# Gathering the next expert's tokens one weight pair earlier and transposing them one pair later

## The chip, the cores and the metric

The kernel runs on one core of a Trainium2 chip. The metric is the device time of one execution in microseconds. The engines are TensorE (PE, with its weight loads as PEld), VectorE (DVE), ScalarE (ACT), GpSimd (POOL) and SyncE (SP), which issues most of the transfers.

## What is computed

One layer of a backbone over 2048 latent tokens and 256 context tokens of width 1024: a mixing sub-layer (a gated convolution beside a bidirectional mLSTM) and then a mixture of 16 experts in which every expert chooses its own 256 tokens. Only the second part matters here; the whole is in float32.

```python
def one_set(hs):                       # hs: (2048, 1024)
    aff = jax.nn.softmax(jnp.einsum('nd,de->en', hs, w_router).astype(jnp.float32), axis=0)
    g, idx = lax.top_k(aff, cap)       # cap = 256 tokens per expert
    xe = hs[idx]
    a = jnp.einsum('ecd,edf->ecf', xe, w_gate)
    u = jnp.einsum('ecd,edf->ecf', xe, w_up)
    ye = jnp.einsum('ecf,efd->ecd', jax.nn.silu(a) * u, w_down) * g[..., None].astype(hs.dtype)
    return jax.ops.segment_sum(ye.reshape(-1, hs.shape[-1]), idx.reshape(-1), num_segments=n)
```

The sum over experts is gated, added to the stream, and a final RMSNorm follows.

## The kernel before

The first stage ends with the normalised tokens and their router weights in a table in memory, XN (2048 rows of 1040 numbers), the stream in ACC, and two small tables, AH and RB, from which the list of an expert's 256 tokens can be made. That takes until about 1160 us. Then the loop over the 16 experts runs, `for e in range(NE)`, with an inner loop over six pairs of 128-wide slices of the expert's hidden width (1408 = 11 slices; the last pair has one).

In each pair, gate and up weights are loaded by SP (load_w, L85), split into a high part on ACT (L92) and a rest on VectorE (L96) and multiplied with the expert's transposed tokens, xh and xl, by 96 matmuls of 256 columns (L1148 to L1150, into psx). The down weights are loaded and split likewise (L1045, L1051, L1053). The 24 down matmuls (L1086 to L1088, into ac) run one pair behind: those of pair 0 are traced in iteration pr = 1, and those of the last pair in pr = 0 of the next expert, followed by finish(), which scales the rows and adds them to ACC by two indirect transfers on POOL's queue (L1110).

While expert e is computed, xprep(e + 1) prepares the next one:

- the one-hot tile oh from ix and AH on VectorE (L1006), 16 index products on TensorE into pi (L1009), a copy to ic (L1011) and the integer indices idx (L1014);
- two indirect gathers from XN into the two tiles gx, 128 rows each, on POOL's queue (L1017);
- the router weights gg from the gathered rows on VectorE (L1021);
- four groups of four transposes on TensorE into ptx (L1032), each group read by ACT (xh, L1035) and VectorE (xf, L1037; xl, L1038), two times in turn.

The PSUM pool ptr has one buffer, which pi and the four groups ptx share. The tile oh has one buffer as well, and the squares eq of early() and finish() use it too (tag "oh"). early(t) normalises rows of ACC that no later expert touches; it runs in the last two experts from pr = 1 on, two row tiles in each pair of expert 14.

The order on each engine isn't written by hand. A planner lays out the instructions by their simulated readiness, and among those that are ready the one traced first goes first; the engines then keep to that order. So the trace place of a call is its priority. All of xprep(e + 1) is called at the end of pr = 2, behind the down matmuls of pair 1:

```python
                if pr == 2 and e + 1 < NE:
                    nxt = xprep(e + 1)
```

Of the kernel before, what the change touches and what calls it, by code (L numbers as in the profile page):

```python
# [25 lines left out]
NE = 16  # L26
# [12 lines left out]
def kernel(ctx, tc, x, c, cx, c_ctx, w_mod, b_mod, g_norm1, g_norm2, w_in, w_out, conv_w, conv_b,  # L39
# [43 lines left out]
    def load_w(src, rows, cols):  # L83
        raw = wrawp.tile([P, rows, cols], F32, name="wraw", tag="wraw")
        nc.sync.dma_start(raw, src)  # L85
        return raw

    def split_w(raw, rows, cols, after=None, after_lo=None):
        hi = whip.tile([P, rows, cols], F32R, name="whi", tag="whi")
        if after is not None:  # L90
            S.activation(hi[:, 0, 0:1], after, AF.Copy)
        S.activation(hi, raw, AF.Copy)  # L92
        lo = whip.tile([P, rows, cols], F32R, name="wlo", tag="wlo")
        if after_lo is not None:
            V.tensor_copy(lo[:, 0, 0:1], after_lo)
        V.tensor_sub(lo, raw, hi.bitcast(F32))  # L96
        return hi, lo
# [150 lines left out]
    for q in range(4):  # L248
        pmf = psm.tile([P, 512], F32, name="pm", tag="sm")
        pm = pmf[:, 0:8].rearrange("p (r i s) -> p r i s", r=2, i=2)  # L250
        for r in range(2):
            pr = pmm.tile([P, 512], F32, name="pr", tag="mm")
# [743 lines left out]
    with tc.tile_pool(name="xw", bufs=2, reuse_waits="tile") as xraw, tc.tile_pool(name="xh", bufs=2, reuse_waits="tile") as xhi, \  # L996
# [2 lines left out]
            tc.tile_pool(name="extr", bufs=1, space=PSUM, reuse_waits="tile") as ptr, \  # L999
            tc.tile_pool(name="exac", bufs=4, space=PSUM, reuse_waits="tile") as pac:  # L1000

        def xprep(e):
            oh = wk.tile([P, P, 16], BF16, name="oh", bufs=1)
            if e == 1:
                V.tensor_copy(oh[:, 0, 0:1], xp[1].bitcast(F32)[:, KD - 1, 0:1])
            V.tensor_tensor(oh, ix, AH[:, e].unsqueeze(1).to_broadcast([P, P, 16]), op=ALU.is_equal)  # L1006
            pi = ptr.tile([P, 512], F32, name="pi", tag="tr")
            for j in range(16):
                T.matmul(pi[:, 0:4], oh[:, :, j], RB[:, e, j], start=j == 0, stop=j == 15)  # L1009
            ic = wk.tile([P, 4], F32, name="ic", bufs=1)  # L1010
            V.tensor_copy(ic, pi[:, 0:4])  # L1011
            idx = wk.tile([P, 2], I32, name="idx", bufs=3)
            icv = ic.rearrange("p (h f) -> p f h", f=2)
            V.scalar_tensor_tensor(idx[:, ::-1], icv[:, 0], float(P), icv[:, 1], op0=ALU.mult, op1=ALU.add)  # L1014
            gxs = [wk.tile([P, XW], F32, name="gx", bufs=2) for _ in range(2)]
            for hf_ in range(2):
                G.indirect_dma_start(out=gxs[hf_], out_offset=None, in_=XN,  # L1017
                                     in_offset=bass.IndirectOffsetOnAxis(ap=idx[:, hf_:hf_ + 1], axis=0))
            gg = wk.tile([P, 2], F32, name="gg", bufs=2)
            for hf_ in range(2):  # L1020
                V.tensor_copy(gg[:, hf_:hf_ + 1], gxs[hf_][:, D + e:D + e + 1])  # L1021
            xh = wk.tile([P, KD, 2 * P], F32R, name="xh", bufs=2)
            xl = wk.tile([P, KD, 2 * P], F32R, name="xl", bufs=2)
            for k2 in range(KD // 2):
                if e == 0:
                    pt = pac.tile([P, 512], F32, name="ac", tag="ac").rearrange("p (i t) -> p i t", i=2)
                else:
                    pt = ptr.tile([P, 2, 2 * P], F32, name="ptx", tag="tr")
                for i in range(2):
                    for hf_ in range(2):  # L1030
                        k = k2 * 2 + i
                        T.transpose(pt[:, i, hf_ * P:(hf_ + 1) * P], gxs[hf_][:, k * P:(k + 1) * P], ident)  # L1032
                for i in range(2):
                    k = k2 * 2 + i
                    S.activation(xh[:, k], pt[:, i], AF.Identity, scale=A2[:, k:k + 1], bias=B2[:, k:k + 1])  # L1035
                    xf = wk.tile([P, 2 * P], F32, name="xf", bufs=2)
                    V.tensor_scalar(xf, pt[:, i], A2[:, k:k + 1], B2[:, k:k + 1], op0=ALU.mult, op1=ALU.add)  # L1037
                    V.tensor_sub(xl[:, k], xf, xh.bitcast(F32)[:, k])  # L1038
            return xh, xl, gg, idx

        def wsplit_d(src, rows, gate=None, after=None, col=None):
            raw = xraw.tile([P, rows, D], F32, name="draw", tag="draw")
            if gate is not None:
                V.tensor_copy(raw[:, 0, 0:1], gate)
            nc.sync.dma_start(raw, src)  # L1045
            if col is not None:
                G.tensor_mul(raw, raw, col.unsqueeze(1).to_broadcast([P, rows, D]))
            hi = xhi.tile([P, rows, D], F32R, name="dhi", tag="dhi")
            if after is not None:
                S.activation(hi[:, 0, 0:1], after, AF.Copy)  # L1050
            S.activation(hi, raw, AF.Copy)  # L1051
            lo = xhi.tile([P, rows, D], F32R, name="dlo", tag="dlo")
            V.tensor_sub(lo, raw, hi.bitcast(F32))  # L1053
            return hi, lo
# [61 lines left out]
                V.tensor_scalar(ar, ar, fr, None, op0=ALU.mult)  # L1116
                G.indirect_dma_start(out=out, out_offset=rows(e, hf_), in_=ar, in_offset=None)

        xp = xprep(0)
        pend = []  # L1120
        for e in range(NE):
            xh, xl, gg, idx = xp
            accs = None
            nxt = None
            for pr in range(npair):
                n = 2 if pr < npair - 1 else NFT - 2 * (npair - 1)
                f0 = pr * 2
                ws = []
                for src in (w_gate_e, w_up_e):
                    raw = load_w(src[0, e][:, f0 * P:(f0 + n) * P].rearrange("(k p) n -> p k n", p=P), KD, n * P)  # L1130
                    if e == 0 and pr == 0:
                        ws.append(split_w(raw, KD, n * P, thr[:, 0:1], idx[:, 0:1]))
                    elif e == 0 and pr == 1 and not ws:
                        ws.append(split_w(raw, KD, n * P, xl.bitcast(F32)[:, 5, 0:1]))
                    else:
                        ws.append(split_w(raw, KD, n * P))
                dw = wsplit_d(w_down_e[0, e][f0 * P:(f0 + n) * P, :].rearrange("(i p) n -> p i n", p=P), n,
                              gg[:, 0:1] if e == 0 and pr < 2 else None,
                              xl.bitcast(F32)[:, KD - 1, 0:1] if e == 0 and pr < 2 else None,
                              ml5b if e == NE - 1 else None)  # L1140
                hts = []
                for i in range(n):
                    ps = pmm.tile([P, 2, 2 * P], F32, name="psx", tag="mm")
                    for m_ in range(2):
                        hi, lo = ws[m_]
                        for k in range(KD):
                            wh = hi[:, k, i * P:(i + 1) * P]
                            T.matmul(ps[:, m_], wh, xh[:, k], start=k == 0, stop=False)  # L1148
                            T.matmul(ps[:, m_], wh, xl[:, k], start=False, stop=False)  # L1149
                            T.matmul(ps[:, m_], lo[:, k, i * P:(i + 1) * P], xh[:, k], start=False, stop=k == KD - 1)  # L1150
                    sgt = wk.tile([P, 2 * P], F32, name="sgt", bufs=2)
                    S.activation(sgt, ps[:, 0], AF.Silu)  # L1152
                    V.tensor_tensor(sgt, ps[:, 1], sgt, op=ALU.mult)  # L1153
                    hh = wk.tile([P, 2 * P], F32R, name="hh", bufs=4)
                    S.activation(hh, sgt, AF.Copy)  # L1155
                    hl = wk.tile([P, 2 * P], F32R, name="hl", bufs=4)
                    V.tensor_sub(hl, sgt, hh.bitcast(F32))  # L1157
                    hts.append((hh, hl))
                last = pr == npair - 1
                if pend and not (e == NE - 1 and last):  # L1160
                    pe, pxp, paccs, ppr, plast = pend.pop()
                    if paccs is None:
                        paccs = [pac.tile([P, 512], F32, name="ac", tag="ac") for _ in range(4)]
                    down(paccs, ppr)
                    if plast:
                        finish(pe, pxp, paccs)
                    else:
                        accs = paccs
                pend.append((e, xp, accs, ([f0 + i for i in range(n)], hts, dw), last))
                if e >= NE - 2 and pr:  # L1170
                    cuts = ((0, 2, 4, 6, 8, 10), (10, 12, 14, 16, 16, 16))[e - NE + 2]
                    for t in range(cuts[pr - 1], cuts[pr]):
                        early(t)
                if pr == 2 and e + 1 < NE:
                    nxt = xprep(e + 1)
            if nxt is not None:
                xp = nxt
        accs = pend[0][2]
# [51 lines left out]
```

## Time and profile before

| | |
|---|---|
| time before, median of 3 runs | 2762.28 us (2760.39 to 2766.7) |
| span of the profiled execution | 2763.4 us |
| TensorE busy | 2641.4 us (96%) |
| VectorE busy | 1605.3 us (58%) |
| ScalarE busy | 1149.4 us (42%) |
| GpSimd busy | 333.2 us (12%) |
| mean granted TensorE clock | 0.983 |

The time of the profiled execution is given by its span; it lies between the fastest and the slowest run shown. Busy times are of one execution. A matmul's listed duration is longer than its share of TensorE's time, since matmuls overlap: what one costs is read from the starts of the ones that follow. A wait is written behind a row as the idle time of its engine and what ended it.

### The profile page before, as it was taken

The numbers are of one execution on the slowest core, as the hardware profiler recorded it, in microseconds if no ns is written. First come the engines' busy times: TensorE is split into PE (matmuls) and PEld (weight loads), VectorE is DVE, ScalarE is ACT, GpSimd is POOL, SyncE is SP. The second block draws the span as 40 slices with busy tenths as digits, with TensorE's granted clock in tenths as the row PEclk, the third lists the DMA queues.
The fourth block names the chain that finished last, engine by engine and source line by source line (L and its number), as shares of the span: only waits on it lengthen the run. The fifth ranks groups of instructions, "written<-read, shape, count | busy, mean of one in ns | idle before, by whom it ended". The sixth has DMA issues, their size and how long they took to land. (4 is left out here: it accounts for less than half of the span.)

```text
span 2763.4 us, 42877 instructions
## 1 busy us (share of the span) xinstructions
PE 2641.4 (96%) x17550; PEld 2378.9 (86%) x17550; DVE 1605.3 (58%) x2603; ACT 1149.4 (42%) x1682; POOL 333.2 (12%) x351
## 2 busy tenths in 40 slices
PE   8999999999999999299999999999999999999987
PEld 5988888888878888299899999999999999999887
DVE  5356454544575665665556555655665565565684
ACT  3243323423434434254444444444444444444443
POOL 1010000000111111300010001001000100100253
PEclk9999999999999999699999999999999999999999
DMA  8444645535565654167567666756756665665965
GB/s 265 134 154 145 188 140 175 183 107 178 201 209 185 200 178 149 61 218 225 176 191 221 194 196 202 219 190 191 221 184 197 207 208 193 198 214 178 304 229 185
DMA packets 382533, 524.57 MB, mean 190 GB/s; under 512 B 15072, under 2 KB 322736, under 8 KB 380288
## 3 DMA queue, kind: packets, MB, share of 16 engines
q1 hardware_dynamic: 327968, 437.96, 48.8%
q10 hardware_dynamic: 43792, 46.55, 5.0%
q0 software_dynamic: 10576, 37.32, 4.9%
q8 instruction: 137, 2.24, 0.3%
q14 instruction: 60, 0.49, 0.1%
HBM read 449.05 MB, written 72.61 MB: 189 GB/s over the span
## 5 line engine op out<-in xcount | busy, mean ns | idle before, releaser
L1148 PE MATMUL psx<-xh,whi 128*128 128x256 f32 x2816 | 793.6, 282 | 0.0
L1150 PE MATMUL psx<-xh,wlo 128*128 128x256 f32 x2816 | 789.4, 280 | 1.3 <-DVE wlo L96 1.3
L1149 PE MATMUL psx<-xl,whi 128*128 128x256 f32 x2816 | 787.8, 280 | 2.1 <-DVE xl L1038 2.1
L96 DVE TENSOR_TENSOR wlo<-wraw,whi 128x2048 fp32r<-128x2048 f32 x248 | 542.1, 2187 | 343.9 <-ACT whi L92 343.7
L92 ACT ACTIVATE whi<-wraw 128x2048 fp32r<-128x2048 f32 x248 | 447.2, 1804 | 394.4 <-PE psx L1149 135.8
L1148 PEld LDWEIGHTS psx<-xh,whi 128*128 128x128 f32 x2816 | 532.1, 189 | 3.2
L1149 PEld LDWEIGHTS psx<-xl,whi 128*128 128x128 f32 x2816 | 530.1, 188 | 5.5 <-DVE xl L1038 2.3
L1150 PEld LDWEIGHTS psx<-xh,wlo 128*128 128x128 f32 x2816 | 530.9, 189 | 2.0 <-DVE wlo L96 1.9
L1088 PE MATMUL ac<-dhi,hl 128*128 128x512 f32 x704 | 278.0, 397 | 4.3 <-DVE hl L1157 4.3
L1086 PE MATMUL ac<-dhi,hh 128*128 128x512 f32 x704 | 278.3, 395 | 0.0
L1087 PE MATMUL ac<-dlo,hh 128*128 128x512 f32 x704 | 278.0, 395 | 0.0
L1053 DVE TENSOR_TENSOR dlo<-draw,dhi 128x2048 fp32r<-128x2048 f32 x96 | 202.7, 2112 | 126.3 <-ACT dhi L1051 126.3
L417 PE MATMUL ps<-hlo,whi 128*128 128x512 f32 (+1 forms) x672 | 259.4, 387 | 0.0
L418 PE MATMUL ps<-hhi,wlo 128*128 128x512 f32 (+1 forms) x672 | 258.9, 386 | 0.0
L416 PE MATMUL ps<-hhi,whi 128*128 128x512 f32 (+1 forms) x672 | 258.4, 387 | 0.0
L1051 ACT ACTIVATE dhi<-draw 128x2048 fp32r<-128x2048 f32 x96 | 170.1, 1773 | 84.0 <-PE ac L1088 84.0
L1110 POOL DMA_INDIRECT ACC<-yv,idx x28 | 82.2, 2937 | 938.9 <-DVE yv L1105 825.8
L1155 ACT ACTIVATE hh<-sgt 128x256 fp32r<-128x256 f32 x176 | 73.1, 417 | 268.3 <-DVE sgt L1153 268.3
L1088 PEld LDWEIGHTS ac<-dhi,hl 128*128 128x128 f32 x704 | 132.2, 188 | 36.8 <-DVE hl L1157 4.5
L1152 ACT ACTIVATE sgt<-psx 128x256 f32<-128x256 f32 x176 | 65.7, 374 | 222.9 <-PE psx L1150 222.9
L1087 PEld LDWEIGHTS ac<-dlo,hh 128*128 128x128 f32 x704 | 132.3, 188 | 28.2
L1086 PEld LDWEIGHTS ac<-dhi,hh 128*128 128x128 f32 x704 | 132.3, 188 | 28.1
(405 smaller groups left out, 3981.7 us busy)
## 6 DMA issues: line engine op xcount, KB each, us to landing
wraw<-in_w_gate_e_dram SPq DMA_DIRECT2D x80, 1024.0 KB, 5.9
wraw<-in_w_up_e_dram SPq DMA_DIRECT2D x80, 1024.0 KB, 5.5
draw<-in_w_down_e_dram SPq DMA_DIRECT2D x80, 1024.0 KB, 5.1
wraw<-in_w_in_dram SPq DMA_DIRECT2D x56, 1024.0 KB, 5.4
pk<-PK SPq DMA_DIRECT2D x16, 1284.0 KB, 7.6
xt<-in_x_dram SPq DMA_DIRECT2D x32, 512.0 KB, 5.3
wraw<-in_w_mod_dram SPq DMA_DIRECT2D x16, 1024.0 KB, 6.9
wm<-in_w_mod_dram SPq DMA_DIRECT2D x8, 1024.0 KB, 12.0
```

The source lines that it names most:

```text
L92: S.activation(hi, raw, AF.Copy)
L96: V.tensor_sub(lo, raw, hi.bitcast(F32))
L416: T.matmul(ps[:, :ntok], wh, his[k], start=k == 0, stop=False)
L417: T.matmul(ps[:, :ntok], wh, los[k], start=False, stop=False)
L418: T.matmul(ps[:, :ntok], lo[:, k, i * P:(i + 1) * P], his[k], start=False, stop=k == KD - 1)
L1053: V.tensor_sub(lo, raw, hi.bitcast(F32))
L1086: T.matmul(ac, hhs, dh[:, i, sl], start=f == 0, stop=False)
L1087: T.matmul(ac, hhs, dl[:, i, sl], start=False, stop=False)
L1088: T.matmul(ac, hls, dh[:, i, sl], start=False, stop=f == NFT - 1)
L1148: T.matmul(ps[:, m_], wh, xh[:, k], start=k == 0, stop=False)
L1149: T.matmul(ps[:, m_], wh, xl[:, k], start=False, stop=False)
L1150: T.matmul(ps[:, m_], lo[:, k, i * P:(i + 1) * P], xh[:, k], start=False, stop=k == KD - 1)
```

## The change

The function xprep is cut in two. xgather(e) holds the one-hot tile, the index products, the indices, the two gathers and the allocation of gg; xprep(e, gth) holds the gg copies, the transposes and their evictions. In the loop xgather(e + 1) is called at the end of pr = 1 and xprep(e + 1, gth) at the end of pr = 3, in place of both at the end of pr = 2. Expert 0 is prepared ahead of the loop by the two calls in a row.

```diff
-        def xprep(e):
+        def xgather(e):
             oh = wk.tile([P, P, 16], BF16, name="oh", bufs=1)
...
             gg = wk.tile([P, 2], F32, name="gg", bufs=2)
+            return gxs, gg, idx
+
+        def xprep(e, gth):
+            gxs, gg, idx = gth
             for hf_ in range(2):
                 V.tensor_copy(gg[:, hf_:hf_ + 1], gxs[hf_][:, D + e:D + e + 1])
...
-        xp = xprep(0)
+        xp = xprep(0, xgather(0))
...
-                if pr == 2 and e + 1 < NE:
-                    nxt = xprep(e + 1)
+                if pr == 1 and e + 1 < NE:
+                    gth = xgather(e + 1)
+                if pr == 3 and e + 1 < NE:
+                    nxt = xprep(e + 1, gth)
```

## Rows read from the trace of the kernel before

**Rows 1.** The page's busy line: engine, busy us, share, instructions.
```profile
PE 2641.4 (96%) x17550; PEld 2378.9 (86%) x17550; DVE 1605.3 (58%) x2603; ACT 1149.4 (42%) x1682; POOL 333.2 (12%) x351
```

**Rows 2.** Waits from 1190 us on: engine, line, releaser: us, times, longest.
```profile
PE ptx L1032 <- DMA gx<-XN,idx: 19.1, 13, 2.8
PE pi L1009 <- DVE oh L1006: 5.0, 1, 5.0
PE psx L1149 <- DVE xl L1038: 2.1, 1, 2.1
PE ptx L1032 <- DVE xf L1037: 1.1, 1, 1.1
...
ACT xh L1035 <- DVE xf L1037: 74.1, 52, 3.1
```

**Rows 3.** TensorE in order of time, one expert: start, us, line, operation, [idle before].
```profile
1709.76 1.15 PE L1009 MATMUL pi<-Cb,oh 128*128 128x4 bf16 x16
...
1719.48 0.30 PE L1032 MATMUL ptx<-ident,gx 128*128 128x128 f32 x1 [1.03 <-DMA gx<-XN,idx]
...
1723.84 0.40 PE L1086 MATMUL ac<-dhi,hh 128*128 128x512 f32 x1
...
1729.44 0.28 PE L1148 MATMUL psx<-xh,whi 128*128 128x256 f32 x1
...
1747.12 0.60 PE L1032 MATMUL ptx<-ident,gx 128*128 128x128 f32 x4
...
1758.59 0.28 PE L1148 MATMUL psx<-xh,whi 128*128 128x256 f32 x1
```

**Rows 4.** Windows: us, busy PE PEld DVE ACT POOL, PEclk, DMA, GB/s.
```profile
1661.84:1673.14 11.30, 11.30 (x97) 11.30 (x96) 3.97 (x5) 4.63 (x4) 0.00 (x0) 1.00 0.65 214
...
2489.00:2504.00 15.00, 13.07 (x98) 12.89 (x97) 5.71 (x8) 4.20 (x7) 3.95 (x2) 0.89 0.33 117
...
2597.00:2607.00 10.00, 10.00 (x70) 10.00 (x71) 5.26 (x8) 3.57 (x5) 3.04 (x5) 0.66 0.83 289
```

**Rows 5.** POOL in order of time: the second scatter and the first gather.
```profile
1687.42 2.78 POOL L1110 DMA_INDIRECT ACC<-yv,idx  x1 [7.78 <-DMA ACC<-yv,idx]
1713.11 2.30 POOL L1017 DMA_INDIRECT gx<-XN,idx  x1 [22.90 <-issue]
```

**Rows 6.** TensorE, ACT and VectorE in order of time, iteration 14.
```profile
2569.94 0.28 PE L1148 MATMUL psx<-xh,whi 128*128 128x256 f32 x1
...
2575.38 1.06 ACT L1062 ACTIVATE eq<-ea 128x1024 bf16<-128x1024 f32 x1 [8.72 <-DMA ea<-ACC]
...
2577.73 0.19 ACT L1062 ACTIVATION_READ_ACCUMULATOR eq<-ea 128x1 f32 x1
...
2578.70 0.42 DVE L1157 TENSOR_TENSOR hl<-sgt,hh 128x256 fp32r<-128x256 f32 x1
...
2595.67 1.22 DVE L1006 TENSOR_TENSOR oh<-ix,UA 128x2048 bf16<-128x2048 bf16 x1
```

**Rows 7.** ACT and VectorE in order of time: reading the last two groups.
```profile
1741.86 0.55 DVE L1037 TENSOR_SCALAR xf<-ptx,A,B 128x256 f32<-128x256 f32 x1 [0.17 <-ACT xh L1035]
...
1750.12 0.56 ACT L1035 ACTIVATE xh<-ptx,B,A 128x256 fp32r<-128x256 f32 x1 [1.30 <-DVE xf L1037]
...
1751.30 0.43 DVE L1038 TENSOR_TENSOR xl<-xf,xh 128x256 fp32r<-128x256 f32 x1
```

**Rows 8.** TensorE in order of time, expert 0: first and last group.
```profile
1225.76 0.60 PE L1032 MATMUL ptx<-ident,gx 128*128 128x128 f32 x4
...
1252.23 0.60 PE L1032 MATMUL ptx<-ident,gx 128*128 128x128 f32 x4
```

**Rows 9.** TensorE in order of time, expert 14: first and last group.
```profile
2613.00 0.27 PE L1032 MATMUL ptx<-ident,gx 128*128 128x128 f32 x1
...
2644.91 0.60 PE L1032 MATMUL ptx<-ident,gx 128*128 128x128 f32 x4
```

**Rows 10.** VectorE in order of time: a weight split late in expert 14.
```profile
2642.47 6.26 DVE L96 TENSOR_TENSOR wlo<-wraw,whi 128x2048 fp32r<-128x2048 f32 x1
```

## The prediction

> **What bounds the kernel now.** I read the page's busy line first, then the waits of TensorE, then the order of time on TensorE inside one expert. The busy line [rows 1] shows TensorE at work for 2641.4 of 2763.4 us and no other engine above 58%, so the kernel gains only what TensorE loses by waiting, about 122 us in all. The waits from 1190 us on, where the expert loop lies [rows 2], tell which part of that this change can touch: 13 waits of the transposes L1032 for the gathered rows (DMA into gx), 19.1 us together, and one wait of the index product L1009 for the one-hot tile oh, 5.0 us. The wait for xl (2.1 us) and that for xf (1.1 us) belong to the same preparation and show what it costs when it comes too late.
>
> The order of time in the expert that prepares from 1709.76 us on [rows 3] shows where the wait comes from. The 16 index products stand right after the down matmuls traced in the third pair; 96 gate and up matmuls of the fourth pair follow, but 63 of them in, at 1719.48, TensorE stands for 1.03 us because the first row tile hasn't landed. The planner had expected it sooner: the gather is issued at 1713.11 [rows 5] and the wait ends at 1719.48, 6.4 us later, while the 63 matmuls fill 7.4 us from the index products' end on. The down matmuls of the fourth pair end at 1729.44, the four groups of transposes reach until 1747.12, and the next expert begins at 1758.59.
>
> **The change part by part.** Nothing is computed more or less: per expert the same 16 index products, two copies to ic and idx, two gathers, two gg copies, 16 transposes, 8 ACT and 16 VectorE evictions. Only the trace place moves, and the place gives the priority by which the planner orders each engine. I take both moves to show in the engines' orders, since the index products stand right behind the down matmuls after which they are traced [rows 3].
>
> *The gather, one pair earlier.* A pair takes 96 matmuls, 11.30 us [rows 4], and 24 down matmuls, 1729.44 - 1723.84 = 5.6 us [rows 3], so 16.9 us. The index products move from 1709.76 to about 1692.9, the two gathers on POOL's queue from 1713.11 to about 1696.2. The queue's neighbour there is the second scatter, busy on POOL from 1687.42 to 1690.2 [rows 5]; it is out of the way, and nothing is queued behind the gather until the next expert's first scatter. The gather takes POOL 2.30 us, so the second follows some 2.6 us behind; even if each took twice the 6.4 us, the second would land near 1712, and the first transposes then stand at 1729.44. The cover is 17 us; without it the old wait of 1 to 2.8 us would return. So the 13 waits go: 19.1 us. With them goes a clock loss: after the wait in the expert at 2487 us the granted clock is 0.89 over 15 us [rows 4], 0.11 x 15 = 1.6 us (both TensorE levels lie in that stretch). And as the first four transposes are no longer split into one and three, a second changeover between transposes and weights goes, about 0.1 us each, 1.3 us. **Gain: 19.1 + 1.6 + 1.3 = 22.0 us.**
>
> The rows say 6.4 us from issue to the end of the wait [rows 3, 5]. [...]
>
> *The transposes, one pair later.* Call t0 the end of the down matmuls of the fourth pair (1729.44 in rows 3). The first group moves from t0 - 10 to t0. How far apart the groups stand is the planner's work: ACT and VectorE have to read one group out of its only PSUM buffer (ptr, one bank), between weight splits of 2 us, before the next group may be written. The span from the first group to the last is 1747.12 - 1719.48 = 27.6 us in the usual expert [rows 3], 26.5 us in expert 0, where the rows are early and the groups begin right after the down matmuls as they will after the change [rows 8], and 31.9 us where expert 15 is prepared [rows 9]. From the last group to the last xl it is 1751.73 - 1747.12 = 4.6 us [rows 3, 7]. So the last xl is ready at t0 + 31.1 (expert 0's spacing) to t0 + 32.2. The next expert begins at 1758.59 - 1729.44 = 29.15 us after t0 [rows 3] plus the fourth group's share of TensorE, of whose 0.60 us in a row of rows 3 I take 0.45, = t0 + 29.6, and needs the last slice of xl as its 23rd matmul, 22 x 0.118 = 2.6 us later: t0 + 32.2. It fits, with 0 to 1.1 us to spare. Bounds per expert: nothing, and 3.1 us (the 1.1 and 2.1 us that TensorE waits in the preparation of expert 15, rows 2, which starts exactly there already, at 2613.00, and whose last group falls after the next expert's start). I take 0.2 us, nearest to expert 0's row, because expert 15 has two things that the others have not: the final normalisation work of early(), and a VectorE split that takes 6.26 us there [rows 10], while POOL multiplies draw (L1047), which it does for no other expert. 14 x 0.2 = **2.8 us lost**, between 0 and 14 x 3.1 = 43 us. Expert 15's own preparation keeps its place. VectorE is also rid of in-order waits for the gather (its gg copies now come after the landing); TensorE doesn't notice that.
>
> *Iteration 14.* The tile oh shares one buffer with the squares eq of early(). Before, oh for expert 15 waited for four of these, now for two, since xgather is traced behind early(0) and early(1). The planner thinks they are done early: ACT stands 8.72 us before the first one, for the load of ACC, and the second ends at 2577.73 + 0.19 = 2577.9 [rows 6]. The comparison that makes oh (1.22 us) follows what VectorE has queued, hl at 2578.70, and ends at about 2578.70 + 0.42 + 1.22 = 2580.3. The planner sees all that some 8.7 us sooner, if ACT's idle time is its error, and so puts the index products near 2571.6, just inside the third pair's matmuls, which start at 2569.94 [rows 6]. So TensorE waits 8.7 us (an estimate; 7.3 if the products stand at 2573, 10.2 if at 2570.1) instead of the 5.0 us [rows 2], which go: **3.7 us lost**. Queued behind on TensorE is the whole third pair. The clock loss after it (0.66 granted over 10 us, rows 4) is there before and after. Below nothing: if the planner puts the product behind the third pair's matmuls, all 5.0 us and the clock loss of 0.34 x 10 = 3.4 us go, 8.4 us gained.
>
> Sum against the profiled execution: 2763.4 - 22.0 + 2.8 + 3.7 = 2747.9 us. Its span lies 1.1 us above the median of the runs shown, 2762.28, so the predicted median is 2747 us, 0.56% faster.
>
> **The rivals.**
> *Preparation too late, slower.* If the last transposes fall into the next expert as they do for expert 15, each of 14 experts pays 3.1 us: 2762.3 - 22.0 + 3.7 + 43.4 = 2787 us. It decides from (22.0 - 3.7) / 14 = 1.3 us per expert on, which is a last group later than about t0 + 28.9. For it speaks that the reserve is only a microsecond, and that ACT's second eviction of a group waits for VectorE's first (1.30 us in rows 7; 52 such waits of 74.1 us in all in rows 2), so that the chain can't be sped up by an idle engine. Against it: the spacings of rows 3 and 8, and that TensorE's order comes from a plan slower than the chip here: the third group's last reader of the buffer is done at 1741.86 + 0.55 = 1742.4 [rows 7], and the last group stands at 1747.12 [rows 3]. [...]
> *The gain is eaten, no change.* If the wait at the next expert's start is 1.1 us on average, the time is 2762.3 - 22.0 + 3.7 + 15.4 = 2759 us. For it: the upper end of my estimate of the last xl already touches the need.
> *The change doesn't do what it says.* The planner might leave TensorE's order as it is, since it places work by readiness; then the time stays at 2762 us. Against it: in the 13 iterations with a wait the index products stand right at their trace place, as in rows 3.
>
> **How the numbers follow.** Forecast 69%, too late 13%, eaten 14%, no effect 4%. About 0.2%, 5.5 us, is what a measurement of this kernel can tell from no change; so faster 69%, same 18%, slower 13%. The low end takes the full 22.0 us with a little back from iteration 14: 2738. The high end takes a wait of 1.3 us in 14 experts and the worst of iteration 14: 2762.3 - 22.0 + 18.2 + 5.2 = 2764. The case of 2787 stays outside, and a little of the others.
>
> **What would show it.** Right: no wait of L1032 for gx but the two of expert 0; index products behind the second pair's down matmuls, gathers some 17 us earlier on POOL; the first group of four transposes together at t0; the last xl before the next expert's 23rd matmul; the single wait for oh in iteration 14 longer, in the third pair. Wrong: waits of L1148 or L1149 for xh or xl at the start of most experts, or last groups that stand after the next expert's first matmul.

## The result

| | before | after |
|---|---|---|
| device time, median | 2762.07 us (2760.39 to 2766.7, 4 runs) | 2748.03 us (2745.0 to 2750.69, 4 runs) |
| span of the profiled execution | 2763.4 us | 2746.3 us |
| 13 whole experts (first matmul of expert 1 to that of expert 14) | 1266.45 us | 1241.71 us |
| the last two experts and the end | 224.48 us | 233.60 us |

The ratio of the times is 0.9949, with a 95% interval from 0.9938 to 0.9961: 0.5% faster. The forecast was 2747 us. The total came out as predicted, but the third and fourth lines of the table show that it is made of a larger gain in the loop and a loss at its end that the prediction doesn't have.

The page of after, its span and its busy line, which answers to [rows 1]:

```profile
span 2746.3 us, 42864 instructions
...
PE 2636.5 (96%) x17550; PEld 2376.2 (87%) x17550; DVE 1606.5 (58%) x2603; ACT 1143.5 (42%) x1682; POOL 338.4 (12%) x351
```

The instructions are the same ones on TensorE; it is busy for 4.9 us less. The waits of after from 1190 us on, which answer to [rows 2]:

```profile
PE ptx L1036 <- DVE xf L1041: 6.4, 1, 6.4
PE pi L1009 <- DVE oh L1006: 5.6, 1, 5.6
PE ac L1092 <- DVE hl L1161: 4.3, 1, 4.3
PE psx L1153 <- DVE xl L1042: 2.1, 1, 2.1
...
DVE gg L1025 <- DMA gx<-XN,idx: 106.0, 28, 7.9
```

(In after the transposes are L1036, their readers xf L1041 and xl L1042, the gate and up matmuls L1152 to L1154, the down matmuls L1090 to L1092; the other lines that the text names keep their work and shift by a few numbers.) The 13 waits of the transposes for gx are gone, and nothing has taken their place in the 13 whole experts: the first two of the waits shown lie in expert 14, the other two in expert 15. The wait of a transpose for xf, 1.1 us before, is now 6.4 us.

TensorE in order of time in one expert of after, which answers to [rows 3]:

```profile
1684.07 1.16 PE L1009 MATMUL pi<-Cb,oh 128*128 128x4 bf16 x16
...
1718.98 0.60 PE L1036 MATMUL ptx<-ident,gx 128*128 128x128 f32 x4
...
1727.78 0.60 PE L1036 MATMUL ptx<-ident,gx 128*128 128x128 f32 x4
...
1736.65 0.60 PE L1036 MATMUL ptx<-ident,gx 128*128 128x128 f32 x4
...
1743.92 0.60 PE L1036 MATMUL ptx<-ident,gx 128*128 128x128 f32 x4
...
1748.57 0.28 PE L1152 MATMUL psx<-xh,whi 128*128 128x256 f32 x1
```

Both trace places show in TensorE's order. The index products stand behind the second pair's down matmuls. The first group of transposes stands right at the end of the fourth pair's, all four together (t0 = 1718.98), and the next expert begins at t0 + 29.6. The four groups take 24.9 us from first to last. VectorE and then POOL in order of time, in the same expert:

```profile
1695.19 0.15 DVE L1025 COPY gg<-gx 128x1 f32<-128x1 f32 x1 [6.37 <-DMA gx<-XN,idx]
...
1748.98 0.42 DVE L1042 TENSOR_TENSOR xl<-xf,xh 128x256 fp32r<-128x256 f32 x1
```

```profile
1678.43 2.98 POOL L1114 DMA_INDIRECT ACC<-yv,idx  x1 [7.56 <-DMA ACC<-yv,idx]
1687.41 2.30 POOL L1017 DMA_INDIRECT gx<-XN,idx  x1 [6.00 <-issue]
```

The gather stands 6 us behind the second scatter on POOL's queue, not in its way, and its rows are there at 1695.19, 23.8 us ahead of t0, those of the second gather at 1697.61, 21.4 us ahead. The last xl is done at 1748.98 + 0.42 = 1749.40, t0 + 30.4; the next expert needs it at 1748.57 + 2.6 = 1751.2.

Now the two stretches. Windows of before, then of after: from:to, length, busy time of PE, PEld, DVE, ACT and POOL with the number of records, granted TensorE clock, DMA share, GB/s.

```profile
1272.47:2538.92 1266.45, 1247.23 (x8997) 1162.13 (x8996) 746.99 (x845) 572.54 (x624) 119.02 (x52) 1.00 0.64 200
2538.92:2763.40 224.48, 197.84 (x1365) 182.92 (x1363) 146.61 (x141) 98.97 (x131) 83.83 (x62) 0.95 0.70 236
```

```profile
1270.99:2512.70 1241.71, 1241.71 (x8998) 1159.53 (x8996) 747.28 (x845) 566.86 (x624) 119.10 (x52) 1.00 0.65 204
2512.70:2746.30 233.60, 201.12 (x1365) 186.00 (x1363) 148.11 (x142) 99.43 (x131) 86.62 (x62) 0.93 0.66 226
```

In the 13 experts of after TensorE is busy in every microsecond, 95.52 us per expert against 97.42. The gain of 1266.45 - 1241.71 = 24.7 us is 1266.45 - 1247.23 = 19.2 us of idle time and 1247.23 - 1241.71 = 5.5 us of busy time. The last two experts lose 9.1 us, and the start of expert 1 lies 1.5 us earlier. That isn't the change: expert 0 already starts 1.6 us earlier, with the same instructions ahead of it (its start varied between 1176.03 and 1179.63 us over all the kernels here), and itself takes 94.3 us against 94.2. Together: -24.7 + 9.1 - 1.5 = -17.1 us, the difference of the two spans.

Where the last two experts lose it: TensorE in order of time, after.

```profile
2553.97 0.29 PE L1009 MATMUL pi<-Cb,oh 128*128 128x4 bf16 x2 [5.63 <-DVE oh L1006]
...
2612.89 0.45 PE L1036 MATMUL ptx<-ident,gx 128*128 128x128 f32 x1 [6.38 <-DVE xf L1041]
...
2630.84 0.38 PE L1153 MATMUL psx<-xl,whi 128*128 128x256 f32 x1 [2.11 <-DVE xl L1042]
```

If the starts of the same matmuls in the two traces are set against each other from expert 14's first one on, after is 0.1 us late when the fifth pair begins, in spite of the longer wait for oh. It falls back by 7.6 us at the third group of transposes, 2612.89, and behind it (the wait of 6.38 against 1.06, and the clock, 0.84 granted over the 15 us from 2613.00 on against 1.00 behind the same group before), and by another 1.5 us in the first pair of expert 15. The rows of VectorE and then of POOL just ahead of that group:

```profile
2600.05 1.28 DVE L1076 SCALAR_TENSOR_TENSOR ea<-ea,fr,ml2b 128x1024 f32<-128x1024 f32 x1 [0.44 <-POOL fr L81]
2602.06 5.65 DVE L1076 SCALAR_TENSOR_TENSOR ea<-ea,fr,ml2b 128x1024 f32<-128x1024 f32 x1 [0.72 <-POOL fr L81]
...
2608.77 0.53 DVE L1041 TENSOR_SCALAR xf<-ptx,A,B 128x256 f32<-128x256 f32 x1
...
2612.21 0.53 DVE L1041 TENSOR_SCALAR xf<-ptx,A,B 128x256 f32<-128x256 f32 x1
```

```profile
2601.99 4.64 POOL L1051 TENSOR_TENSOR draw<-draw,ml5b 128x2048 f32<-128x2048 f32 x1
```

The same operation on the same shape takes 1.28 us and then 5.65, in the stretch in which POOL multiplies the last expert's down weights. The two xf that read the transposes out of their one PSUM buffer are queued behind it on VectorE, and the third group waits for them.

That alone isn't new. In the kernel before, the same multiply already stood beside a VectorE row ahead of the same two xf, and the third group waited 1.06 us. VectorE and then POOL, before:

```profile
2624.86 4.85 DVE L1157 TENSOR_TENSOR hl<-sgt,hh 128x256 fp32r<-128x256 f32 x1
2629.64 0.53 DVE L1037 TENSOR_SCALAR xf<-ptx,A,B 128x256 f32<-128x256 f32 x1
...
2633.08 0.54 DVE L1037 TENSOR_SCALAR xf<-ptx,A,B 128x256 f32<-128x256 f32 x1
```

```profile
2624.55 4.88 POOL L1047 TENSOR_TENSOR draw<-draw,ml5b 128x2048 f32<-128x2048 f32 x1 [2.73 <-DMA out_dram<-ea]
```

What differs is where all this lies. Counted from the first matmul of expert 14 (2538.92 before, 2512.70 after), the first group of transposes stands at 74.1 us before and at 73.9 after: it has kept its place. The multiply begins at 85.6 before and at 89.3 after, and the second of the two xf at 94.2 before and at 99.5 after, while TensorE is ready for the third group at 93.8 in both.

### The profile page after: what moved, and what is told of

It is laid out like the page before. It is cut to its first block, busy times and chain, and to the rows that moved or that the text cites. A ratio compares the mean times of both kernels' runs of the same rounds, so it can differ in the third digit from the quotient of the medians.

```text
span 2746.3 us, 42864 instructions
## 1 busy us (share of the span) xinstructions
PE 2636.5 (96%) x17550; PEld 2376.2 (87%) x17550; DVE 1606.5 (58%) x2603; ACT 1143.5 (42%) x1682; POOL 338.4 (12%) x351
## 5 line engine op out<-in xcount | busy, mean ns | idle before, releaser
L1154 PE MATMUL psx<-xh,wlo 128*128 128x256 f32 x2816 | 788.6, 280 | 1.1 <-DVE wlo L96 1.1
L1152 PE MATMUL psx<-xh,whi 128*128 128x256 f32 x2816 | 789.1, 281 | 0.0
L1154 PEld LDWEIGHTS psx<-xh,wlo 128*128 128x128 f32 x2816 | 530.8, 189 | 1.9 <-DVE wlo L96 1.8
L1152 PEld LDWEIGHTS psx<-xh,whi 128*128 128x128 f32 x2816 | 529.8, 189 | 2.5
L1092 PE MATMUL ac<-dhi,hl 128*128 128x512 f32 x704 | 278.4, 397 | 4.3 <-DVE hl L1161 4.3
L1090 PE MATMUL ac<-dhi,hh 128*128 128x512 f32 x704 | 280.9, 399 | 0.0
L1159 ACT ACTIVATE hh<-sgt 128x256 fp32r<-128x256 f32 x176 | 73.2, 417 | 299.6 <-DVE sgt L1157 299.6
L1092 PEld LDWEIGHTS ac<-dhi,hl 128*128 128x128 f32 x704 | 132.7, 189 | 36.6 <-DVE hl L1161 4.6
L1090 PEld LDWEIGHTS ac<-dhi,hh 128*128 128x128 f32 x704 | 133.1, 189 | 27.2
```

What stands on the lines that cost most here:

```text
L1090: T.matmul(ac, hhs, dh[:, i, sl], start=f == 0, stop=False)
L1092: T.matmul(ac, hls, dh[:, i, sl], start=False, stop=f == NFT - 1)
```

## The experiments

The theory after the result: the loop's gain needs only distance between gather and transposes, so either half of the change would bring it; and the loss at the end comes from POOL's multiply, beside which a VectorE row of 1.28 us takes 5.65, ahead of the evictions of expert 15's transposes. The rivals: that the halves need each other; that the loss comes from the wait for oh, which moved a pair ahead; and that the transposes are already at the latest place they can have.

The measured values of all kernels (each group of runs had its own runs of the kernel before; the stretches are those of the windows above):

| kernel | median, us | ratio to before, 95% | 13 experts | last two and end |
|---|---|---|---|---|
| after | 2748.03 | 0.9949 [0.9938, 0.9961] | 1241.71 | 233.60 |
| gather_early | 2734.58 | 0.9893 [0.9876, 0.9909] | 1240.54 | 222.10 |
| transposes_late | 2738.36 | 0.9905 [0.9888, 0.9921] | 1241.71 | 221.83 |
| old_in_14 | 2739.47 | 0.9909 [0.9892, 0.9925] | 1241.71 | 223.54 |
| no_mul | 2734.32 | 0.9892 [0.9876, 0.9909] | 1241.71 | 218.30 |
| mul_on_dve | 2751.4 | 0.9951 [0.9934, 0.9968] | 1241.71 | 233.49 |
| pr0_in_14 | 2734.06 | 0.9892 [0.9874, 0.9909] | 1241.72 | 218.19 |
| ge_pr0_14 | 2734.63 | 0.9892 [0.9875, 0.9908] | 1240.55 | 221.80 |
| pr0_pr1_in_14 | 2735.88 | 0.9906 [0.989, 0.9923] | 1241.71 | 220.51 |
| transposes_pr4 | 2809.99 (one run) | | 99.38 per expert | |

### One half of the change alone: gather_early and transposes_late

The gather at pr = 1 with the transposes where they were:

```diff
-                if pr == 3 and e + 1 < NE:
+                if pr == 2 and e + 1 < NE:
                     nxt = xprep(e + 1, gth)
```

> The first half alone: index products and gather at the end of the second pair, transposes back at the end of the third. Theory A (the gain of the loop is the cover of the gather's 6 us, and either half gives it): no wait of the transposes for gx after expert 0, an expert from 2 to 13 takes 95.5 us as in the changed kernel, against 97.4 before. In iteration 14 the wait for oh stays in the third pair (5.6 us), the groups of expert 15 start 17 us earlier than in the changed kernel, so its waits of 6.4 us for xf and 2.1 us for xl should go: 2738 to 2742 us. Theory B (the later place of the transposes gives the gain, because they no longer meet the weight splits of the fourth pair): waits of some 1.5 us an expert remain, 97 us an expert, about 2760 us.

And the transposes at pr = 3 with the gather where it was:

```diff
-                if pr == 1 and e + 1 < NE:
+                if pr == 2 and e + 1 < NE:
                     gth = xgather(e + 1)
```

> The second half alone: index products and gather stay at the end of the third pair, the transposes go to the end of the fourth. Theory A: the gather lands some 8.5 us behind the index products and the transposes stand 16.9 us behind them, so the 13 waits go here too and an expert takes 95.5 us; in iteration 14 the wait for oh is where it was before (5.0 us) and expert 15 is prepared as in the changed kernel: 2745 to 2750 us. Theory that the gather has to be a whole pair early to be covered: waits of about 1 us an expert stay, 2755 to 2762 us.

Both halves take the whole gain in the 13 experts, 25.9 and 24.7 us, and neither has the loss at the end (222.10 and 221.83 us, against 224.48 before). So one pair of distance is enough; the second one, which after has, buys nothing (1241.71 us, as transposes_late, and 1.2 us more than gather_early). Each half alone beats the change (0.9893 and 0.9905 against 0.9949). Both times are below what I had expected, 2738 to 2742 and 2745 to 2750 us: I had taken the loss at the end to stay where the transposes are late, and it doesn't. In gather_early the last transposes for expert 15 stand at 2594.1 us, ahead of the multiply at 2599.86, so none of them can wait for an eviction that it holds up. In transposes_late the multiply (from 2601.21, 4.61 us) lies beside another VectorE row than in after: an xl, 0.42 us elsewhere, takes 4.86 us, and a transpose waits 1.8 us for xf instead of 6.4.

VectorE in order of time, transposes_late:

```profile
2601.25 4.86 DVE L1042 TENSOR_TENSOR xl<-xf,xh 128x256 fp32r<-128x256 f32 x1
```

So the late place of the transposes alone doesn't make the loss; which VectorE operation stands beside the multiply, and when, has a part in it.

### The loss at the end: old_in_14, no_mul, mul_on_dve

Expert 14 as before, the other experts as after:

```diff
-                if pr == 1 and e + 1 < NE:
+                if pr == (1 if e < NE - 2 else 2) and e + 1 < NE:
                     gth = xgather(e + 1)
-                if pr == 3 and e + 1 < NE:
+                if pr == (3 if e < NE - 2 else 2) and e + 1 < NE:
                     nxt = xprep(e + 1, gth)
```

> The change for experts 0 to 13, but in iteration 14 both halves at the end of the third pair as before. Theory C (the 9 us that the last two experts lost come from the places of expert 15's preparation): the wait for xf falls from 6.4 us to the 1.1 us of before and the last two experts take 9 us less, 2739 us. Rival (they come from where POOL's multiply of draw happens to fall, whatever the place): it may fall on VectorE's evictions again, 2745 to 2750 us.

2739.47 us, as expected. The last two experts take 223.54 us, those of before 224.48, and the third group waits 1.0 us for xf, though the multiply stands beside an hl of 4.86 us ahead of its evictions there too: the loss belongs to the order in iteration 14, as the two theories both have it. Which part of that order, the next two kernels are to tell. The first leaves out the multiplication of the last expert's down weights:

```diff
-                              ml5b if e == NE - 1 else None)
+                              None)
```

> The changed kernel without the six multiplies of draw by the gate row in the last expert (its result lacks that factor), nothing else. Theory D in its clean form (POOL's multiply holds VectorE up beside it): the VectorE rows of 5.65 and 6.26 us fall to 1.3 and 2.3 us and TensorE's waits for xf, xl and hl in the last two experts, 12.8 us with 2 to 4 us of lost clock, shrink to 3 us: the stretch from the start of expert 14's matmuls to the end falls from 233.6 to some 221 us, 2735 us in all. Rival (the early normalisation and the order of the squares make the preparation late by themselves): the stretch stays over 229 us, 2744 us or more.

Waits of TensorE in no_mul, last two experts:

```profile
PE pi L1009 <- DVE oh L1006: 5.6, 1, 5.6
PE ptx L1036 <- DVE xf L1041: 2.2, 1, 2.2
PE ac L1092 <- DVE hl L1161: 2.2, 1, 2.2
```

VectorE in order of time, no_mul:

```profile
2602.97 1.28 DVE L1076 SCALAR_TENSOR_TENSOR ea<-ea,fr,ml2b 128x1024 f32<-128x1024 f32 x1 [0.71 <-POOL fr L81]
...
2605.32 0.54 DVE L1041 TENSOR_SCALAR xf<-ptx,A,B 128x256 f32<-128x256 f32 x1
```

TensorE's order is the same from end to end, and VectorE's until some 50 rows before its last; the wait for oh is the same 5.6 us, and yet the last two experts take 218.30 us instead of 233.60. The second ea takes 1.28 us again, xf comes 2.35 us after its start instead of 6.71, and the wait of the third group falls from 6.4 to 2.2 us. So of the 5.3 us that this wait has more than before, 4.1 hang on the multiply, and 1.2 don't. Expert 14 takes 104.45 us before, 112.02 after and 106.48 in no_mul. The other 9.8 of the 15.3 us lie in expert 15 and the end (121.58 in after, 111.82 in no_mul), where the multiplies cost something before as well ([rows 10]; 120.03 us).

Why the multiply costs 1.0 us in one order and 6.4 in another is to be read by setting the kernels side by side, in us from the first matmul of expert 14:

| | before | old_in_14 | transposes_late | gather_early | after | no_mul |
|---|---|---|---|---|---|---|
| index products of expert 15 | 58.0 | 58.0 | 58.3 | 41.1 | 41.3 | 41.3 |
| first group of transposes | 74.1 | 74.0 | 73.3 | 57.6 | 73.9 | 73.2 |
| early()'s squares traced at pr = 4 | 78.8 | 78.7 | 78.9 | 84.1 | 85.0 | 84.5 |
| first multiply of draw on POOL | 85.6 | 85.5 | 86.8 | 89.0 | 89.3 | none |
| third group of transposes | 94.8 | 94.7 | 94.9 | 75.8 | 100.2 | 95.3 |
| its wait for xf | 1.1 | 1.0 | 1.8 | none | 6.4 | 2.2 |
| length of expert 14 | 104.5 | 104.3 | 104.5 | 103.1 | 112.0 | 106.5 |

Where the gather is traced at pr = 1, early()'s squares of pr = 4 stand 5 to 6 us later and the multiply 2 to 4 us later. In gather_early the transposes are over by then. In transposes_late they stand where they do in after, but the multiply is earlier. Only the two halves together put the late multiply ahead of evictions that TensorE waits for. Why early()'s tiles come later isn't shown. TensorE's wait for oh isn't itself the loss, since no_mul has it too and TensorE has caught up by the fifth pair; whether it is what delays the tiles stays open.

The same multiply on VectorE instead of POOL, as a way to keep it without the collision:

```diff
-                G.tensor_mul(raw, raw, col.unsqueeze(1).to_broadcast([P, rows, D]))
+                V.tensor_mul(raw, raw, col.unsqueeze(1).to_broadcast([P, rows, D]))
```

> The changed kernel with the six multiplies of draw by the gate row of the last expert on VectorE instead of POOL, nothing else. Theory D (POOL's multiply holds VectorE up for its 4.6 to 8 us, and that is what makes TensorE wait for xf, xl and hl in the last two experts): the long VectorE rows of 5.65 and 6.26 us fall to 1.3 and 2.3 us, the waits of 6.4, 2.1 and 4.3 us shrink to 3 us together, and the time falls by 8 to 12 us with the clock, to 2736 to 2740 us, though VectorE has some 13 us more work there. Rival (the early normalisation alone makes it late): the waits stay, and with VectorE's extra work the time is 2748 to 2755 us.

This gave nothing, 2751.4 us, in the range of the rival. Waits of TensorE in mul_on_dve, last two experts:

```profile
PE psx L1153 <- DVE xl L1042: 9.3, 3, 6.2
PE pi L1009 <- DVE oh L1006: 5.5, 1, 5.5
PE psx L1152 <- DVE sgt L1157: 5.2, 1, 5.2
```

The long rows are gone (ea takes 1.28 us, wlo 2.29), but the multiplies, 2.28 us each, now stand in VectorE's own order, which the planner lays out anew, and the waits come back as 9.3 us for xl and 5.2 us for sgt, all of them in the last expert: expert 14 takes 102.6 us, 9.4 less than in after, and the rest 130.9, 9.3 more. It is no test of the collision, since it changes the order as well; no_mul is.

### Other places in iteration 14: pr0_in_14, pr0_pr1_in_14, ge_pr0_14

If oh is traced ahead of early()'s first squares, the wait for oh should go too. After, with expert 15's gather at pr = 0 and its transposes at pr = 2:

```diff
-                if pr == 1 and e + 1 < NE:
+                if pr == (1 if e < NE - 2 else 0) and e + 1 < NE:
                     gth = xgather(e + 1)
-                if pr == 3 and e + 1 < NE:
+                if pr == (3 if e < NE - 2 else 2) and e + 1 < NE:
                     nxt = xprep(e + 1, gth)
```

> The change for experts 0 to 13; in iteration 14 index products and gather at the end of the first pair, ahead of the early normalisation, and the transposes at the end of the third pair. Theory C (the places in iteration 14 carry the loss): oh no longer waits for the squares, so the wait of 5.6 us for oh goes with the 3 us of clock behind it, the groups of expert 15 stand a pair earlier and the waits for xf and xl go: the last two experts take 217 to 221 us instead of 233.6, 2732 to 2736 us. Rival (the early normalisation then holds up something else in the same pairs by as much): 2740 us or more.

2734.06 us, as expected: the wait for oh is gone and the last two experts take 218.19 us. With the transposes at pr = 1 in iteration 14 (the second line `3 if e < NE - 2 else 1`):

> The change for experts 0 to 13; in iteration 14 the gather at the end of the first pair and the transposes at the end of the second, so that the last preparation is over before POOL's first multiply of draw. Theory E (what is left of the loss with the gather at the first pair is VectorE's evictions of expert 15 meeting early() and the multiply): the waits for xf of 1.0 us and xl go, those of the last expert for hl, whi and wlo (7.7 us together) stay, as they hang on the multiply: 2730 to 2733 us. Rival (every place only shifts the collision): 2734 us or more.

2735.88 us, above the range, the last stretch 220.51: the waits for xf and xl are gone and most of those on the multiply stay, as expected, but the transposes are too early now, one wait of 2.9 us for gx has come back. And gather_early with the gather of iteration 14 at pr = 0, the kernel that by the sum of the two findings should have been the fastest:

```diff
-                if pr == 1 and e + 1 < NE:
+                if pr == (1 if e < NE - 2 else 0) and e + 1 < NE:
                     gth = xgather(e + 1)
-                if pr == 3 and e + 1 < NE:
+                if pr == 2 and e + 1 < NE:
                     nxt = xprep(e + 1, gth)
```

> Transposes at the end of the third pair for all experts, gather at the end of the second, in iteration 14 at the end of the first. By theory A and C: 95.4 us an expert in the loop as with the gather moved alone, and in iteration 14 no wait of 5.4 us for oh and no clock loss after it: 2733 - 5.4 - 2 to 3 = 2725 to 2729 us, below both kernels. Rival (VectorE is held by the squares' load there anyway and the wait returns at hl or xl): 2732 to 2736 us.

2734.63 us, no better than gather_early. The wait for oh went, but the last stretch is 221.80 us against 222.10: a transpose waits 3.0 us for xf, down matmuls 3.1 for hl, gate and up matmuls 3.7 for wlo. Taking one wait away lets the planner's order run into the next; as far as the waits show it, what binds in these two experts is shared by several operations, most of them on VectorE.

### How much reserve the transposes have: transposes_pr4

After with the transposes one more pair later:

```diff
-                if pr == 3 and e + 1 < NE:
+                if pr == 4 and e + 1 < NE:
                     nxt = xprep(e + 1, gth)
```

> The changed kernel with the transposes at the end of the fifth pair instead of the fourth, 11.7 us of TensorE's work before the next expert. By the prediction's reckoning the last xl is ready 30.4 us after the first group and is needed 2.6 us into the next expert: 11.7 + 0.5 x 4 + 2.6 = 16 us, so some 14 us are missing in each of 15 experts, less what the down matmuls of the last pair (2.8 us) and faster groups take back: 6 to 12 us an expert, 2840 to 2930 us. Rival (the groups can follow each other every 3 us when the next expert waits for them, so that 12 us are enough): a loss of under 3 us an expert, below 2790 us.

Eleven experts of transposes_pr4, first the window, then TensorE's waits in it:

```profile
1339.59:2432.75 1093.16, 1070.92 (x7613) 997.77 (x7612) 631.11 (x715) 479.21 (x528) 61.44 (x44) 0.99 0.65 196
```

```profile
PE psx L1153 <- DVE xl L1042: 21.7, 13, 1.8
```

An expert takes 1093.16 / 11 = 99.38 us, 3.9 more than in after: 2.0 us idle (1093.16 - 1070.92 = 22.24, by 11), nearly all of it the wait for xl of the rival "too late", and 1.8 us of busy time. It costs more than the 1.9 us per expert that the change gains, and the kernel is 1.6% slower than before (2809.99 us in one run, against 2764.57): the 13 experts take 23.6 us more than before, and the last two and the end 22.9 us more, with waits for xl of up to 6.6 us. The rival's mechanism is real, and its place is one pair behind the change. I had expected more; the four groups stand closer together there (1356.50, 1364.00, 1372.04 and 1377.52 us in the first such expert, 21.0 us instead of 24.9).

## Why the prediction was right, and where it was not

**The gather, one pair earlier.** Right in mechanism: the index products behind the second pair, the gather 16.9 us earlier in the expert (34.4 us from its start instead of 51.3), clear of the scatter, and no wait for gx. The size was 24.7 us instead of 22.0: beside the 19.1 us of idle I put 2.9 us of clock and changeovers, and the busy time fell by 5.5 us. The rest can be found in the trace of before. The row ahead of the waiting transpose in [rows 3]:

```profile
1718.16 0.28 PE L1150 MATMUL psx<-xh,wlo 128*128 128x256 f32 x1
```

Unhindered, the next instruction starts 0.12 us after this one, but its listed end is 0.28 us after, and the idle time is counted from there. Over the 13 waits the transposes started 21.15 us later than they would have (1.32 - 0.12 in this one), not 19.1: 2.1 us of the waits are listed as busy. The other 39 changes from psx to ptx took 0.14 us on average before, against the 0.12 that two psx stand apart: 0.8 us. (After has 13 such changes, at 0.12; its other groups follow a down matmul.) And the clock:

```profile
2439.39:2538.92 99.53, 97.60 (x693) 91.09 (x692) 56.91 (x65) 43.96 (x48) 9.48 (x4) 0.98 0.62 196
```

That is the last of the 13 experts of before, with 0.98 granted (0.50 to 0.52 from 2498 to 2501 us, in windows of 1 us, and 1.00 before that and from 2502 us on); in after it has 1.00. It is busy for 97.60 us, an expert of after for 95.52; less the 0.16 of its wait that is listed as busy and 0.08 for its second changeover, that is 1.8 us, near the estimate (1.6). The second changeover shows behind the transposes: the first psx behind a ptx is followed 0.202 us later, where two psx stand 0.117 apart (averages of after), 65 times in the 13 experts of before and 39 times in after; 13 times in after it is a down matmul, followed 0.32 us later instead of 0.23. So before has 13 more of these steps, 13 x 0.085 = 1.1 us, near the estimate (1.3). From start to next start the 208 transposes take 18.30 us before, split, and 18.45 after. Together 2.1 + 0.8 + 1.8 + 1.1 - 0.15 = 5.65 us, against 5.5 measured.

**That both moves are needed** I didn't say, but I added their terms as if the gain came from the gather's move alone. The runs show that either half does it: transposes_late leaves the gather at its place, and its 13 experts take the same 1241.71 us.

**The transposes, one pair later.** The estimate of t0 + 31.1 to 32.2 for the last xl was on the safe side: t0 + 30.4, because the groups stand 24.9 us apart from first to last, not 26.5 to 27.6. The start of the next expert, t0 + 29.6, came out to the tenth. So the term of 2.8 us is 0, the reserve is 1.8 us and not 0 to 1.1, and the rivals "too late" and "eaten" are false here; transposes_pr4 shows the first one where it begins.

**Iteration 14's wait for oh.** The sign was right and the size wrong: 5.6 us, 38 matmuls into the third pair, instead of 8.7 us some 14 in. I took ACT's whole idle time ahead of the first squares (8.72 us, [rows 6]) for the planner's error; the planner had put the products later than that. The net is 0.6 us, not 3.7, and when the fifth pair begins 0.1 us of it is left.

**"Expert 15's own preparation keeps its place."** This is the step that failed. Its transposes do keep their place (74.1 and 73.9 us into expert 14), but I gave no term to what stands beside them. With the gather a pair earlier and the transposes where they are, early()'s tiles of pr = 4 come 6.2 us later, POOL's multiply 3.7 us later, and the eviction that the third group needs 5.3 us later. I had the row that warns of it, the wlo of 6.26 us beside the multiply [rows 10], and used it to say why expert 15 is a bad guide for the others, but not to ask what the change does to expert 15. It lost 7.6 us there and 1.5 us behind it. no_mul shows that most of the wait hangs on the multiply, and transposes_late and gather_early that it takes both halves; why early()'s tiles come later, and what the 1.5 us are, stays open.

**VectorE "rid of in-order waits for the gather"** was wrong: the gg copies, traced at pr = 3, stand at 1695.19, a pair ahead of their trace place, and VectorE waits longer for them than before (106.0 us in 28 waits, 80.8 in 26). TensorE doesn't notice, as I wrote: in the 13 experts of after it is busy for all of the 1241.71 us, VectorE for 747.28.

**The sum.** Predicted -22.0 + 2.8 + 3.7 = -15.5 us; the spans say -24.7 + 9.1 - 1.5 = -17.1, the medians -14.0. The total was right because a gain too small and two losses too large (by 2.7, 2.8 and 3.1 us) stand against a loss of 8.5 us that I didn't see. The medians differ by less than the spans: I compared the span of before with the median of device times. After's profiled run took 2748.26 us for a span of 2746.3, 2.0 us more; if it was so before, its profiled execution lay some 3 us above its median.

**Open.** Why the last two experts of the various orders end between 218 and 224 us was followed only for the waits named above. Whether some other mix of places in experts 14 and 15 gets below 218 us wasn't tried. A version that keeps the multiply on POOL but moves it out of VectorE's way wasn't tried either.

## What to carry to other kernels

When a preparation is moved in a loop, walk through each iteration that differs from the rest (here the one with the final normalisation and the scaled weights) and ask what is now beside it; the 14 alike gave what they promised, and the odd one took back over a third (9.1 of 24.7 us). Try each half of a two-part move alone: here either half brings the whole gain, and each alone was faster (1.1% and 1.0% against 0.5%). The listed waits of the transposes were a little shorter than the delays (19.1 us against 21.15 over the 13 here), since they are counted from the listed end of the matmul before, 0.28 us after its start, where the next one starts 0.12 us after it.

## What the hardware showed that was not expected

Three VectorE rows ended only after the multiply of draw that POOL had begun before them. The scalar_tensor_tensor on 128x1024 took 5.65 us instead of 1.28 beside the 4.64 us multiply that began 0.07 us before it, and ended 1.08 us after it, nearly its own whole time. An xl of 0.42 us took 4.86 in transposes_late, beside a multiply of 4.61 that began 0.04 us before it; the wlo of [rows 10] took 6.26 us, 2.29 in mul_on_dve where the multiply isn't on POOL. The multiply beside that wlo, before:

```profile
2641.04 5.54 POOL L1047 TENSOR_TENSOR draw<-draw,ml5b 128x2048 f32<-128x2048 f32 x1 [2.46 <-DMA draw<-in_w_down_e_dram]
```

The wlo, xl and ea rows all read two tiles in SBUF; an xf, which reads one operand of this size, from PSUM, began at 2642.02 us before, beside the same multiply as the wlo, and kept its 0.54 us. The ea and the wlo took about what was left of the multiply and their own time together: 4.57 + 1.28 = 5.85 us against 5.65, and 4.11 + 2.29 = 6.40 against 6.26. So in these rows they look held up until the multiply's end rather than slowed by a share; by what isn't shown. It went the other way round too: in gather_early a multiply that began at 2619.55 us, 0.13 us behind a dlo of 2.28 us, took 6.62 us, about the 2.15 us that were left of the dlo and its own 4.6.
